# Hybrid SSD, RWKV-7 and mLSTM layer: a later shuffle and more row tiles in the RWKV part, B and C made there, two branch gates between the last mLSTM heads, layer norm copies on two engines

## The chip, the cores and the metric

The kernel runs on 1 core of one Trainium2 chip. The metric is the device time in microseconds (us) of one execution; the time before is the median of three runs. Engine names are those of the profile: PE is TensorE (PEld its weight loads), DVE is VectorE, ACT is ScalarE, POOL is GpSimd, SP is SyncE, which only issues DMAs here.

## The reference: what is computed

One decoder layer over 256 positions of 2048 channels, all float32. `h` is the layer norm of the input. One projection `w_in` feeds three causal mixers and three sigmoid gates; the gated sum of the three branches goes through `w_out`, and a gated MLP with a short causal convolution follows.

```python
def hybrid_mixer(h, w_in, ...):
    proj = h @ w_in
    (ssd_z, ssd_xbc, ssd_dt, rwkv_p, ml_qk, ml_v, ml_o, ml_i, ml_f,
     gate_pre) = jnp.split(proj, IN_SPLITS, axis=-1)
    ...
    g_ssd, g_rwkv, g_mlstm = jnp.split(jax.nn.sigmoid(gate_pre), N_BRANCHES, axis=-1)
    merged = (g_ssd * (y_ssd @ proj_ssd) + g_rwkv * (y_rwkv @ proj_rwkv)
              + g_mlstm * (y_mlstm @ proj_mlstm))
    return merged @ w_out

def reference(x, ...):
    h = layer_norm(x, ln_in_g, ln_in_b)
    h = layer_norm(DEEPNORM_ALPHA * h + hybrid_mixer(h, ...), ln1_g, ln1_b)
    return layer_norm(DEEPNORM_ALPHA * h + conv_ffn(h, ...), ln2_g, ln2_b)
```

In the SSD mixer (Mamba-2), the columns `xbc` go through a convolution of width 4 and a SiLU, and are split into x, B and C; B and C are 512 columns each. The RWKV-7 mixer keeps a 64x64 state in each of 32 heads, with its update `S_t = S_(t-1) diag(w_t) + (S_(t-1) a_t) b_t^T + v_t k_t^T` and `y_t = S_t r_t`. The mLSTM has 8 heads with a running maximum.

## The kernel before, in words

**Weights.** The kernel streams every weight matrix once from HBM. A chunk (`wraw`) holds two row tiles, that is 2 x 128 rows of 512 columns. ACT casts it to the high half `whi` (L163 in the RWKV part, L239 elsewhere), DVE subtracts to get the low half `wlo` (L164, L240), and PE multiplies hi by hi, lo by hi and hi by lo, each in a reduced float32 format. A block of 512 columns has 16 row tiles. In `cm_units` (L256, L258, L260; the result has channels on the partitions) a row tile is 12 matmuls of 128x256; in `tm_units` (L278 to L280; time on the partitions) it is 6 matmuls of 128x512. "Tile" below is such a row tile.

**Layer norm to channels.** `to_cm` transposes the normalised rows on PE (L309), scales into the high half on ACT (L314), scales again into a copy `tocm` on DVE (L315) and subtracts to get the low half `xl` (L317). It runs twice: ahead of `w_in` and ahead of the FFN. `affine_tm` multiplies and adds the norm's vectors to the rows that stay in time order, on POOL (L360), with vectors that SP loads as `gb`.

**The RWKV part** stands in a `manual_schedule`: PE, DVE, ACT and POOL run in the order in which the program issues. Two generators are zipped: `groups()` issues the steps of four groups of heads and yields a number, and for each such number so many elements of `weights()` are issued: one tile of a block, or nothing (`yield False`) while a block waits for a page of SBUF. So each `yield n` puts n tiles of weights between two steps. `weights()` walks through `order`: the k, v and r blocks of groups 1 to 3, then gates, 26 blocks of 16 tiles. A v block's result needs the page that the tail of the group two before has read. `Ahead` loads four chunks ahead and cuts so that two chunks (four tiles) beyond the one in use are cut.

For each group g: `pre(g)` makes decay, a, and the normalised k (LoRA matmuls L628, head sums L670, `nk` L684 and L685); `pairs(g)` makes the pair matrices (L741) and transposes bk (L752); `inverse(g)` inverts a triangular matrix: DVE transposes it (L770), POOL runs a chain of small steps (L783, L785), the shuffle (L808) and two stream transposes (L810, L812) on DVE take its result, and PE goes on with it (L823, L833). Inside that generator stand also the transposes of v (L791), and the norm of k times v (L797 to L806). `tail(g-1)`, woven into it, normalises the group before and transposes it (L925 to L955; PE at L945). `recurrence(g)` is PE's (L856, L867).

**After it.** `ssd_bc` makes B and C: a `cm` block each, the first step of the convolution on ACT (L384), three more for each of four column tiles on DVE (L387), a SiLU on ACT (L969). Then the SSD groups, the projections of RWKV and SSD with their gates (`branch`, merged on POOL at L1146), the mLSTM (`ml_in`, `ml_head`: matmuls L1092, L1093 and L1104; the transposes of its result `mn` at L1158), its projection, `w_out`, and the FFN. In these parts a scheduler orders the instructions by their dependences. A gate's block ends in a sigmoid (L1130) and a store to DRAM on ACT's queue (L1131); `branch` loads it again.

The lines of the changed kernel lie some 10 to 31 further on: L628 is L659 there, L752 is L783, L770 is L801, L808 to L812 are L839 to L843, L823 is L854, L925 to L955 are L956 to L986, L384 is L390, L387 is L396, L1158 is L1180, L1104 is L1126, L360 is L363, and L583 is the new SiLU of B and C.

## Time and profile before

| what | value |
|---|---|
| time, median of 3 runs | 2452.67 us (2452.11 to 2454.07) |
| the profiled execution, its own time | 2451.87 us |
| its span (first to last instruction) | 2450.1 us |
| mean granted clock of PE | 0.984 |
| PE busy | 2369.3 us (97%) |
| DVE, ACT, POOL busy | 1546.7, 1247.3, 509.5 us |
| DMA | 447.66 MB, mean 183 GB/s |

How to read the profile: one execution on the chip was recorded. An engine is busy from the start of an instruction to its end; time between is idle, and the trace names what released the engine (`L164` is line 164 of the kernel, `wlo` the tile). "PE acc L279 <- DVE wlo L164" reads: PE's matmul of line 279 waited for the subtraction of line 164 on DVE. PEclk is the share of full clock that TensorE was granted; 0.5 is half. In a table of stretches each row is from:to in us, then length, PE busy, the number of PE instructions, granted clock, DMA share and GB/s.

### The profile page before, as it was taken

What the parts mean: (1) busy time and instruction counts of PE and PEld (TensorE: products, weight loads), DVE (VectorE), ACT (ScalarE), POOL (GpSimd) and SP (SyncE); (2) the same over time, 40 slices, a digit from 0 to 9 for tenths busy, and PEclk for the clock granted to TensorE, in tenths of its full rate; (3) what the DMA queues carried; (4) which work ended last, traced back from release to release, by engine and by line L of the source; (5) the groups of instructions that cost most, each with busy time, mean ns of one, the idle gap of its engine ahead of it and who ended that gap; (6) DMA issues with size and microseconds to landing.
All of it is one profiled execution on the core that took longest, in us unless ns stands there. A gap on an engine that the chain in (4) does not pass through costs nothing.

```text
span 2450.1 us, 41499 instructions
## 1 busy us (share of the span) xinstructions
PE 2369.3 (97%) x16602; PEld 2131.2 (87%) x16602; DVE 1546.7 (63%) x1856; ACT 1247.3 (51%) x1648; POOL 509.5 (21%) x512
## 2 busy tenths in 40 slices
PE   7999998999999999999999998999999999999997
PEld 7898797798777899998889987787999999998886
DVE  6685575676674566786555666557766666665445
ACT  4554654556464555665434566444555455454333
POOL 0046255264363011423010001301200000000000
PEclk9899999999999999999999999999999999999999
DMA  8445454555565776665766664755655655557664
GB/s 241 144 147 164 140 158 147 154 155 164 148 186 164 213 229 179 183 190 190 263 218 188 174 181 155 238 190 175 189 182 185 185 181 182 186 169 234 194 195 148
DMA packets 283730, 447.66 MB, mean 183 GB/s; under 512 B 25816, under 2 KB 118416, under 8 KB 283152
## 3 DMA queue, kind: packets, MB, share of 16 engines
q1 hardware_dynamic: 280368, 433.99, 58.1%
q10 hardware_dynamic: 2592, 8.91, 0.9%
q8 instruction: 130, 2.13, 0.4%
q0 software_dynamic: 576, 2.10, 0.2%
q14 instruction: 64, 0.52, 0.1%
HBM read 430.19 MB, written 14.72 MB: 182 GB/s over the span
## 4 chain that ended last, share of the span: by engine, by line
PE 83%; POOL 6%; DVE 4%; ACT 3%; DMA 2%; issue 2%; SPq 0%; DVEq 0%; ACTq 0%; POOLq 0%
PE acc L256 13%; PE acc L260 13%; PE acc L258 13%; PE acc L278 13%; PE acc L279 12%; PE acc L280 12%; POOL yi L785 3%; POOL si L783 2%; POOL res L360 1%; DVE wlo L164 1%; PE mix L741 1%; ACT whi L163 1%; DVE wlo L240 1%; PE mix L628 1%; PE mix L1023 1%
## 5 line engine op out<-in xcount | busy, mean ns | idle before, releaser
L240 DVE TENSOR_TENSOR wlo<-wraw,whi 128x1024 fp32r<-128x1024 f32 (+2 forms) x548 | 703.3, 1284 | 519.5 <-ACT whi L239 514.2
L239 ACT CAST whi<-wraw 128x1024 fp32r<-128x1024 f32 (+2 forms) x548 | 569.6, 1041 | 656.5 <-PE acc L280 298.9
L256 PE MATMUL acc<-xh,whi 128*128 128x256 f32 x3104 | 885.1, 286 | 4.9 <-ACT whi L239 2.9
L260 PE MATMUL acc<-xh,wlo 128*128 128x256 f32 x3104 | 881.3, 284 | 5.0 <-DVE wlo L164 4.5
L258 PE MATMUL acc<-xl,whi 128*128 128x256 f32 x3104 | 880.9, 284 | 2.8 <-DVE xl L317 2.8
L256 PEld LDWEIGHTS acc<-xh,whi 128*128 128x128 f32 x3104 | 597.3, 193 | 9.2 <-ACT whi L239 3.5
L260 PEld LDWEIGHTS acc<-xh,wlo 128*128 128x128 f32 x3104 | 596.9, 192 | 7.9 <-DVE wlo L164 5.8
L258 PEld LDWEIGHTS acc<-xl,whi 128*128 128x128 f32 x3104 | 597.7, 193 | 4.8 <-DVE xl L317 3.7
L164 DVE TENSOR_TENSOR wlo<-wraw,whi 128x1024 fp32r<-128x1024 f32 x208 | 278.6, 1351 | 239.1 <-ACT whi L163 238.9
L163 ACT CAST whi<-wraw 128x1024 fp32r<-128x1024 f32 x208 | 216.7, 1049 | 118.3 <-PE acc L280 58.3
L279 PE MATMUL acc<-wlo,xh 128*128 128x512 f32 x640 | 255.5, 399 | 9.9 <-DVE wlo L164 9.8
L278 PE MATMUL acc<-whi,xh 128*128 128x512 f32 x640 | 262.1, 414 | 0.1
L280 PE MATMUL acc<-whi,xl 128*128 128x512 f32 x640 | 253.9, 397 | 0.0
L279 PEld LDWEIGHTS acc<-wlo,xh 128*128 128x128 f32 x640 | 122.9, 192 | 34.5 <-DVE wlo L164 12.0
L278 PEld LDWEIGHTS acc<-whi,xh 128*128 128x128 f32 x640 | 122.4, 191 | 29.5 <-issue 1.2
L280 PEld LDWEIGHTS acc<-whi,xl 128*128 128x128 f32 x640 | 122.9, 192 | 26.3
L279 PE MATMUL acc<-wlo,ah 128*128 128x512 f32 x322 | 125.4, 389 | 0.2 <-DVE wlo L240 0.2
L280 PE MATMUL acc<-whi,al 128*128 128x512 f32 x322 | 125.3, 389 | 0.0
L1236 POOL TENSOR_TENSOR fc<-fc 128x512 f32<-128x512 f32 (+1 forms) x22 | 27.9, 1268 | 453.0 <-DVE fc L387 445.0
L278 PE MATMUL acc<-whi,ah 128*128 128x512 f32 x322 | 111.9, 389 | 0.0
L785 POOL TENSOR_TENSOR yi<-yi,si 128x126 f32<-128x126 f32 (+22 forms) x124 | 84.9, 684 | 9.7
L387 DVE SCALAR_TENSOR_TENSOR fc<-acc,fcols,fc 128x255 f32<-128x255 f32 (+1 forms) x172 | 77.0, 478 | 14.0 <-ACT fc L384 12.5
(357 smaller groups left out, 3025.6 us busy)
## 6 DMA issues: line engine op xcount, KB each, us to landing
wraw<-in_w_in SPq DMA_DIRECT2D x368, 512.0 KB, 3.7
wraw<-in_ffn_w_up SPq DMA_DIRECT2D x336, 256.0 KB, 3.0
wraw<-in_ffn_w_down SPq DMA_DIRECT2D x84, 512.0 KB, 4.4
wraw<-in_proj_rwkv SPq DMA_DIRECT2D x32, 512.0 KB, 4.2
wraw<-in_proj_ssd SPq DMA_DIRECT2D x32, 512.0 KB, 4.5
wraw<-in_proj_mlstm SPq DMA_DIRECT2D x32, 512.0 KB, 4.5
wraw<-in_w_out SPq DMA_DIRECT2D x32, 512.0 KB, 4.2
gdram<-gate ACTq DMA_DIRECT2D x16, 512.0 KB, 3.4
```

The source lines that it names most:

```text
L163: nc.scalar.copy(out=hi, in_=self.raw[i])
L164: nc.vector.tensor_tensor(out=lo, in0=self.raw[i], in1=hi.bitcast(F32), op=ALU.subtract)
L239: nc.scalar.copy(out=hi[:, :n, :width], in_=r)
L240: nc.vector.tensor_tensor(out=lo[:, :n, :width], in0=r, in1=hi[:, :n, :width].bitcast(F32), op=ALU.subtract)
L256: nc.tensor.matmul(a, lhsT=wh[:, o:o + m], rhs=X.h(kt), start=st, stop=False, skip_group_check=True)
L258: nc.tensor.matmul(a, lhsT=wh[:, o:o + m], rhs=X.l(kt), start=False, stop=False, skip_group_check=True)
L260: nc.tensor.matmul(a, lhsT=wl[:, o:o + m], rhs=X.h(kt), start=False, stop=kt == nkt - 1, skip_group_check=True)
L278: nc.tensor.matmul(acc[tt], lhsT=X.h(kt)[:, s], rhs=wh, start=kt == 0, stop=False)
L279: nc.tensor.matmul(acc[tt], lhsT=X.h(kt)[:, s], rhs=wl, start=False, stop=False)
L280: nc.tensor.matmul(acc[tt], lhsT=X.l(kt)[:, s], rhs=wh, start=False, stop=kt == nkt - 1)
L387: nc.vector.scalar_tensor_tensor(out=dst[:, j:], in0=ps[:, :T - j], scalar=v(wname, (width - 1 - j) * nch + ct), in1=dst[:, j:], op0=ALU.m ...
L785: gps.tensor_tensor(out=Yo[:, j + 1:32, :e], in0=Yo[:, j + 1:32, :e], in1=tv, op=ALU.subtract)
```

## The change

- `to_cm`: the copy `tocm` has four buffers, not two; PSUM banks come from two tags in turn; of the two column tiles of a step the first is scaled on ACT, the second on DVE.
- `groups()` starts with `yield 8`: eight tiles come ahead of `pre(0)`.
- In `pre` two tiles become three ahead of `nk`; in `inverse` three become four ahead of the norm's sums, and 24 become 27 ahead of the shuffle; in `tail` four become five ahead of the transposes.
- B and C are two new blocks at the end of `order`; `bc_units` issues their convolutions and SiLU in the hand-written order. `ssd_bc` is gone.
- The gates (2, 2) and (2, 3) leave that order and are issued, as ordinary blocks, after heads 6 and 7 of the mLSTM, with pages of their own.
- `affine_tm(r, "ln1")` is issued after the POOL product of the FFN's step c == 8, no longer ahead of the FFN's first matmul.

```diff
     def to_cm(self, n, gname, bname, X):
-            ps = self.bank().rearrange("p (a t) -> p a t", a=2)
+            ps = self.bank("seq" if kt % 4 else "mix").rearrange("p (a t) -> p a t", a=2)
...
-            tmp = self.pg("s%d" % (kt // 2 % 2), [P, 2, T], "tocm")
+            tmp = self.pg("s%d" % (kt // 2 % 4), [P, 2, T], "tocm")
...
-                nc.vector.tensor_scalar(out=tmp[:, a], in0=ps[:, a], scalar1=g, scalar2=b,
-                                        op0=ALU.mult, op1=ALU.add)
+                if a:
+                    nc.vector.tensor_scalar(out=tmp[:, a], in0=ps[:, a], scalar1=g, scalar2=b,
+                                            op0=ALU.mult, op1=ALU.add)
+                else:
+                    nc.scalar.activation(out=tmp[:, a], in_=ps[:, a], func=AF.Identity, scale=g, bias=b)
...
+    last_gates = [(2, 2), (2, 3)]
+
+    def bc_units(self, nm):
+        cts, _ = yield from self.cm_units(self.a["w_in"], [(0, COL[nm], 512)], [(P * j, P) for j in range(4)],
+                                          self.X)
+        while ("pairs", 3) not in self.done:
+            yield False
+        i = "BC".index(nm)
+        t = self.p4(i, "bc")
+        for j in range(4):
+            self.conv_first(cts[j], t[:, j], "scw", 24, 16 + 4 * i + j, 4, "scb", self.v)
+        for j in range(4):
+            yield False
+            self.conv_rest(cts[j], t[:, j], "scw", 24, 16 + 4 * i + j, 4, self.v)
+        yield False
+        self.nc.scalar.activation(out=t, in_=t, func=AF.Silu)
+        self.BC.append(t)
...
-        later = [(i, j) for i in (0, 2, 3) for j in range(NB)]
+        later = [(i, j) for i in (0, 2, 3) for j in range(NB) if (i, j) not in self.last_gates]
...
-        order += [(1, 3)] + later
+        order += [(1, 3)] + later + [("B", 0), ("C", 0)]
...
         def groups():
+            yield 8
             yield from self.pre(0)
...
         self.split(nrr[:, 0], nrr[:, 1], nr)
-        yield 2
+        yield 3
...
         vec.tensor_tensor(out=sql, in0=sq, in1=sqh.bitcast(F32), op=ALU.subtract)
-        yield 3
+        yield 4
...
-        yield 24
+        yield 27
         vec.stream_shuffle(out=Yc[:, :, :, 1], in_=Yo, mask=[i % 16 + 16 for i in range(32)])
...
         vec.tensor_tensor(out=yv, in0=yv, in1=sv.unsqueeze(2).to_broadcast([P, 16, 64]), op=ALU.mult)
-        yield 4
+        yield 5
...
                 self.ml_head(h, qk[h // 4][:, h % 4], qk[2 + h // 4][:, h % 4], Y)
+                if j == 3:
+                    whole(self.gate_units(*self.last_gates[h % 2], page=10 + h % 2))
...
         self.acb = self.p4(18, "acb")
-        self.ssd_bc()
...
         self.to_cm(lambda tt, j: r[j][:, tt], "ln1_g", "ln1_b", X)
-        self.affine_tm(r, "ln1")
...
-            nc.gpsimd.tensor_tensor(out=u, in0=u, in1=t[1][:, :n], op=ALU.mult)
+            m = nc.gpsimd.tensor_tensor(out=u, in0=u, in1=t[1][:, :n], op=ALU.mult)
+            if c == 8:
+                with self.tc.issue_after(m.ins):
+                    self.affine_tm(r, "ln1")
```

Where the edits move instructions, the engines' order in the compiled program shows it. First DVE at the inverse of group 1, where the tail of group 0 is woven in. Before, subtractions of weights (L164) stand between the steps of the tail (L925 to L933) and the norm (L799):

```order
L164 TENSOR_TENSOR wlo_3710<-wraw_3669,whi_3709 128x1024
L770 STREAM_TRANSPOSE ni_3742<-dg_3737 128x1024
L164 TENSOR_TENSOR wlo_3814<-wraw_3707,whi_3813 128x1024
L925 TENSOR_REDUCE hsm_3829<-yt_2647 128x16
L926 TENSOR_SCALAR hsm_3829<-hsm_3829 128x16
L927 TENSOR_TENSOR yt_2647<-yt_2647,hsm_3829 128x1024
L164 TENSOR_TENSOR wlo_3866<-wraw_3811,whi_3865 128x1024
L799 TENSOR_TENSOR sql_3882<-sq_2968,sqh_3881 128x1024
L164 TENSOR_TENSOR wlo_3902<-wraw_3863,whi_3901 128x1024
L933 TENSOR_REDUCE hsm_3929<-y2_3896 128x16
L164 TENSOR_TENSOR wlo_3934<-wraw_3899,whi_3933 128x1024
```

After, from the same transpose on (L801; the tail is L956 to L986):

```order
L801 STREAM_TRANSPOSE ni_3892<-dg_3887 128x1024
L956 TENSOR_REDUCE hsm_3961<-yt_2743 128x16
L957 TENSOR_SCALAR hsm_3961<-hsm_3961 128x16
L958 TENSOR_TENSOR yt_2743<-yt_2743,hsm_3961 128x1024
L830 TENSOR_TENSOR sql_3984<-sq_3076,sqh_3983 128x1024
L964 TENSOR_REDUCE hsm_3989<-y2_3986 128x16
L837 TENSOR_TENSOR v_2150<-v_2150,mix_3992 128x512
L837 TENSOR_TENSOR v_2150<-v_2150,mix_3998 128x512
L968 RECIPROCAL hsm_3989<-hsm_3989 128x16
L969 TENSOR_TENSOR yt_2743<-yt_2743,hsm_3989 128x1024
L985 TENSOR_TENSOR yo_4006<-yo_4006,v_1406 128x1024
L986 TENSOR_TENSOR yo_4006<-yo_4006,gg_3162 128x1024
```

What moved: the subtractions are gone from among these steps. They stand together, two ahead of the transpose and the next behind L986 and the v block's last steps.

Next ACT at B. Before, in `ssd_bc`, the casts of the chunks of C (L239) stand between the first steps of the convolution (L384) and the SiLU (L969):

```order
L384 ACTIVATE bc_8874<-acc_8632,cst_81 128x256
L239 CAST whi_8956<-wraw_8954 128x1024
L384 ACTIVATE bc_8874<-acc_8633,cst_81 128x256
L239 CAST whi_8986<-wraw_8984 128x1024
L384 ACTIVATE bc_8874<-acc_8632,cst_81 128x256
L239 CAST whi_9016<-wraw_9014 128x1024
L384 ACTIVATE bc_8874<-acc_8633,cst_81 128x256
L239 CAST whi_9046<-wraw_9044 128x1024
L239 CAST whi_9076<-wraw_9074 128x1024
L969 ACT_TABLE_LOAD
L969 ACTIVATE bc_8874<-bc_8874 128x1024
L239 CAST whi_9106<-wraw_9104 128x1024
```

After, in the RWKV part, between B's first steps (L390) and its SiLU (L583), with the tail of group 3 (L961, L966) among them:

```order
L163 CAST whi_8529<-wraw_8493 128x1024
L296 CAST yrh_11266<-yl_11283 128x512
L390 ACTIVATE bc_8557<-acc_8250,cst_81 128x256 x2
L390 ACTIVATE bc_8557<-acc_8251,cst_81 128x256 x2
L961 ACTIVATE y2_8562<-yt_7903 128x1024
L966 ACT_TABLE_LOAD
L966 ACTIVATE hsm_8570<-hsm_8570,cst_81 128x16
L583 ACT_TABLE_LOAD
L583 ACTIVATE bc_8557<-bc_8557 128x1024
L163 CAST whi_8584<-wraw_8527 128x1024
```

What moved: `whi_8529` is C's second chunk and `whi_8584` its third; no cast stands between the two.

Last PE at the mLSTM's last two heads. Before, the transposes of head 6's result (L1158), the next head's scores (L1092, L1093) and products (L1104) stand with few weight matmuls among them:

```order
L280 MATMUL acc_14905<-whi_14981,yml_12818 128x512
L280 MATMUL acc_14906<-whi_14981,yml_12818 128x512
L1158 MATMUL mix_14628<-cst_81,mn_14598 128x128
L1092 MATMUL mix_14798<-mqk_13325,mqk_13845 128x256
L1093 MATMUL mix_14798<-mqk_13325,mqk_13845 128x128
L1158 MATMUL mix_14628<-cst_81,mn_14598 128x128 x3
L1104 MATMUL mix_14806<-mvt_14637,mes_14802 128x258
L1104 MATMUL mix_14806<-mvt_14638,mes_14802 128x258
```

After, around the first transpose of the last head's result (L1180), with the matmuls of the third projection (L278 to L280) ahead of it and behind it:

```order
L279 MATMUL acc_14905<-wlo_14964,ymh_12515 128x512
L280 MATMUL acc_14905<-whi_14963,yml_12517 128x512
L278 MATMUL acc_14906<-whi_14963,ymh_12515 128x512
L279 MATMUL acc_14906<-wlo_14964,ymh_12515 128x512
L280 MATMUL acc_14906<-whi_14963,yml_12517 128x512
L278 MATMUL acc_14905<-whi_14981,ymh_12516 128x512
L279 MATMUL acc_14905<-wlo_14982,ymh_12516 128x512
L280 MATMUL acc_14905<-whi_14981,yml_12518 128x512
L1180 MATMUL mix_14736<-cst_81,mn_14706 128x128
L278 MATMUL acc_14906<-whi_14981,ymh_12516 128x512
```

What moved: the heads' steps stand apart, with the tiles of the two gates and of the projection between them.

More of the change, by code (lines that the diff above doesn't have):

```diff
@@ L46 @@
 C_GATE = C_MI + 16
-COL = {"r": C_R, "k": C_K, "v": C_V}
+COL = {"r": C_R, "k": C_K, "v": C_V, "B": C_B, "C": C_C}
 def gate_column(i, j):
@@ L382, in conv, with conv_first, conv_rest @@
     def conv(self, ps, dst, wname, nch, ct, width, bname, v=None):
-        nc, v = self.nc, v or self.v
-        nc.scalar.activation(out=dst, in_=ps, func=AF.Identity,
-                             scale=v(wname, (width - 1) * nch + ct), bias=v(bname, ct))
+        self.conv_first(ps, dst, wname, nch, ct, width, bname, v or self.v)
+        self.conv_rest(ps, dst, wname, nch, ct, width, v or self.v)
+    def conv_first(self, ps, dst, wname, nch, ct, width, bname, v):
+        self.nc.scalar.activation(out=dst, in_=ps, func=AF.Identity,
+                                  scale=v(wname, (width - 1) * nch + ct), bias=v(bname, ct))
+    def conv_rest(self, ps, dst, wname, nch, ct, width, v):
+        nc = self.nc
         for j in range(1, width):
@@ L556, in rkv_units @@
         self.t[nm, g] = t
+    last_gates = [(2, 2), (2, 3)]
[14 more added lines that the diff above has]
+        self.BC.append(t)
     def rwkv(self):
         nc, tc, W = self.nc, self.tc, self.a["w_in"]
-        self.t, self.g_, self.done = {}, {}, set()
+        self.t, self.g_, self.done, self.BC = {}, {}, set(), []
         self.lw = self.load_lora(0)
@@ L585, in weights @@
                     yield from self.rkv_units(g, "r", 0, ("pairs", g - 1))
+                elif a in ("B", "C"):
+                    yield from self.bc_units(a)
                 else:
@@ L958, in tail @@
         yield 1
-    def ssd_bc(self):
-        nc, W = self.nc, self.a["w_in"]
-        self.BC = []
-        for i, c0 in enumerate((C_B, C_C)):
-            cts, _ = self.block_cm(W, c0, self.X)
-            t = self.p4(i, "bc")
-            for j in range(4):
-                self.conv(cts[j], t[:, j], "scw", 24, 16 + 4 * i + j, 4, "scb")
-            nc.scalar.activation(out=t, in_=t, func=AF.Silu)
-            self.BC.append(t)
     def ssd_group(self, g, Y):
@@ L1122, in ml_head, with gate_units @@
             self.split_scaled(ps[:, i], self.v("ml_nw", ct), Y.h(ct), Y.l(ct))
-    def gate_units(self, i, j):
+    def gate_units(self, i, j, page=18):
         acc = yield from self.tm_units(self.a["w_in"], gate_column(i, j), self.X)
-        g = self.pg("p18", [P, 2, 512], "gate")
+        g = self.pg("p%d" % page, [P, 2, 512], "gate")
         for tt in range(2):
```

## Prediction

> **What bounds the kernel now.** I read the page first, then the waits of TensorE, then a table of stretches around the longest of those waits. The page's rows are the busy time of PE, its granted clock in 40 slices and the chain that ended last:
>
> ```profile
> PE 2369.3 (97%) x16602; PEld 2131.2 (87%) x16602; DVE 1546.7 (63%) x1856; ACT 1247.3 (51%) x1648; POOL 509.5 (21%) x512
> PEclk9899999999999999999999999999999999999999
> PE 83%; POOL 6%; DVE 4%; ACT 3%; DMA 2%; issue 2%; SPq 0%; DVEq 0%; ACTq 0%; POOLq 0%
> ```
>
> PE is busy for 2369.3 of 2450.1 us, so some 81 us are all that better order can win in idle time, and the slower clock after a wait adds to that. The matmuls stay the same in number. The change can only close waits of PE or open new ones. PE's waits (engine, what it waited for, us in total, times, longest):
>
> ```profile
> PE acc L279 <- DVE wlo L164: 9.8, 4, 4.8
> PE seq L823 <- DVE x L810: 5.7, 1, 5.7
> PE mix L1158 <- DVE mn L1116: 5.0, 1, 5.0
> PE mix L1158 <- POOL merged L1146: 3.1, 1, 3.1
> PE acc L258 <- DVE xl L317: 2.8, 3, 1.4
> PE mix L309 <- DVE tocm L315: 2.7, 3, 1.1
> PE mix L528 <- DVE s_gs L514: 1.8, 1, 1.8
> ```
>
> The table of stretches gives start and end, length, PE busy with its count, granted clock, DMA share and GB/s:
>
> ```profile
> 91.60:111.90 20.30, 15.52 (x73) 0.66 0.32 106
> 228.50:241.10 12.60, 9.29 (x82) 0.59 0.39 126
> 349.20:404.70 55.50, 47.12 (x379) 0.97 0.54 162
> 404.70:411.80 7.10, 7.03 (x76) 0.51 0.35 88
> 535.70:541.50 5.80, 4.02 (x21) 0.71 0.59 165
> 617.50:626.80 9.30, 7.71 (x54) 0.82 0.55 170
> 752.90:766.80 13.90, 9.10 (x81) 0.63 0.56 189
> 1500.80:1525.70 24.90, 17.30 (x75) 0.86 0.56 167
> 1554.80:1562.10 7.30, 4.25 (x16) 0.77 0.81 262
> 1691.10:1731.00 39.90, 31.93 (x231) 0.91 0.40 110
> 1800.00:1900.00 100.00, 100.00 (x836) 1.00 0.60 185
> 2300.00:2400.00 100.00, 100.00 (x443) 1.00 0.61 194
> ```
>
> The last two rows give the price of a row tile. A tile of 12 matmuls (channel-major) costs 12 x 100/836 = 1.44 us, one of 6 (token-major) 6 x 100/443 = 1.35 us. Each other row is a wait and its wake: length less busy is idle, and the clock costs between busy x (1 - clock) and length x (1 - clock).
>
> **The change part by part.**
>
> *Later shuffle, groups 0 and 3.* The shuffle needs GpSimd's chain, and two stream transposes follow it. DVE's rows at group 3 (start, us, in brackets the idle time before and who ended it):
>
> ```profile
> 751.60 0.01 DVE L808 LOAD_MASK_SELECT yi<-yi  x1 [4.63 <-POOL yi L785]
> 751.60 1.30 DVE L808 STREAM_SHUFFLE yi<-yi 128x512 f32<-128x512 f32 x1
> 752.94 2.00 DVE L810 STREAM_TRANSPOSE x<-yi 128x1024 f32<-128x1024 f32 x1
> 754.84 1.85 DVE L812 STREAM_TRANSPOSE xt<-yi 128x1024 f32<-128x1024 f32 x1
> ```
>
> DVE stands 4.63 + 5.1 us, and the subtractions that make the low half of the weights are queued behind. Two chunks are cut ahead, four tiles, 5.8 us, and PE runs dry. In program order group 0 now has 32 instead of 28 tiles between the norm and the inverse, group 3 has 43 instead of 39 tiles from the last bk transpose: 5.8 us more for POOL, above the 4.63 waited. What stays is 5.1 us of DVE, under the 5.8 us of lead. Group 0: idle 3.3 and clock 3.8 to 5.2, I take 7.5 (4 to 8). Group 3: idle 4.8 and clock 3.4 to 5.1, I take 9 (4 to 9.5).
>
> *The same in group 1: a loss.* Between the last bk transpose and the inverse 23 tiles stand now, 30 before. The v block has used up its 16 tiles, its page waits for the tail of group 0, and no tile stands until that tail's transposes.
>
> ```profile
> 355.11 2.10 DVE L770 STREAM_TRANSPOSE ni<-dg 128x1024 f32<-128x1024 f32 x1 [1.04 <-ACT dg L768]
> 373.62 1.23 DVE L954 TENSOR_TENSOR yo<-yo,v 128x1024 f32<-128x1024 f32 x1 [2.84 <-POOL si L783]
> 401.23 0.01 DVE L808 LOAD_MASK_SELECT yi<-yi  x1 [8.44 <-POOL yi L785]
> ```
>
> The stretch 349.2 to 404.7 ends by GpSimd (8.44 us of DVE waiting for it), so it keeps its length with less put into it: 7 x 1.44 = 10.1 us of weights move behind it. The tail's chain from 355.11 to 373.62 tells where the hole is. It could be less, if the chain shortens with fewer subtractions on DVE, or more if the clock is low behind the hole: -10 (-6 to -14).
>
> *Small steps (one tile more ahead of the nk matmuls, the norm and the tail).* The rows at 535.7 and 617.5 hold 1.8 + 1.6 us of idle and 2.6 to 3.4 of clock. One tile (1.44 us) covers most: +6 (2 to 7).
>
> *Eight tiles ahead of the first pre().* The row at 91.6 holds 4.8 us idle and 5.3 to 6.9 of clock. The eight tiles (11.5 us) go between and behind the small matmuls, so LoRA matmuls no longer stand with nothing behind them. The 1.8 us wait of L528 and some clock may stay: +7.5 of 10.1 (5 to 10). Why some clock: at 535.7 a single wait of 1.8 us was enough for a mean clock of 0.71. [...]
>
> *B and C in the RWKV stretch.* Their matmuls move, at no price. What they bring is a convolution and a SiLU in the hand-written order. Rows of before, where the scheduler spread the same steps:
>
> ```profile
> 893.32 0.56 ACT L384 ACTIVATE bc<-acc,cst 128x256 f32<-128x256 f32 x1
> 905.00 1.28 ACT L969 ACT_TABLE_LOAD   x1
> 906.29 1.06 ACT L969 ACTIVATE bc<-bc 128x1024 f32<-128x1024 f32 x1
> 907.25 1.03 ACT L239 CAST whi<-wraw 128x1024 fp32r<-128x1024 f32 x1
> 893.45 1.23 DVE L240 TENSOR_TENSOR wlo<-wraw,whi 128x1024 fp32r<-128x1024 f32 x1
> 894.59 1.38 DVE L387 SCALAR_TENSOR_TENSOR bc<-acc,cst,bc 128x253 f32<-128x253 f32 x3
> ```
>
> B's SiLU stands on ACT ahead of the cast of C's third chunk, and waits for 12 convolution steps (4 x 1.38 = 5.5 us) with a reduction among them (about 1.2, an estimate from the subtraction's row). The table loads (1.28 each) are over by then. That is 0.6 for the first step on ACT, 5.5 and 1.2, 7.3 in all; SiLU 1.06, cast 1.03 and subtraction 1.23 make 10.6 us after B's last matmul. PE has C's first four tiles, 5.8 us, so it idles some 4 us and then meets a low clock (4.5, as at 228.5): -8.5 (-3 to -12). With two gates fewer, the SSD's first loads of acb come into the last recurrence, on SP between weight loads; they wait for the last gate's store, and ACT's exponentials for them. Before:
>
> ```profile
> 879.96 0.69 ACT L1015 ACTIVATE es<-acb,atm 128x128 f32<-128x128 f32 x2 [2.71 <-DMA acb<-acd]
> ```
>
> ACT waited 2.71 us there and PE did not. Now a cast for B's last chunks stands behind: 0 to -3, I take 0, as four tiles are cut (5.8 us).
>
> *Two gates between the last mLSTM heads.* At 1500.8 PE stands 7.6 us for the last two heads and loses 2.4 to 3.5 to the clock; 16 token-major tiles after each of them (21.7 us) are free of the heads' chains: +10 (7 to 11). The gates' stores stand on ACT's queue behind their sigmoids, and nothing reads them before the third branch. GpSimd then ends the input norm's multiplies under the last gate and the merge isn't queued among them: the row at 1554.8 goes, 3.05 idle and 1.0 to 1.7 of clock: +4 (2 to 5).
>
> *Layer norm copies on two engines.* To_cm's waits are 2.7 + 2.8 us (L315, L317), and 2.9 of clock in the row at 1691.1 (busy x 0.09). Four buffers and two banks' tags take most, the first wait of the FFN stays: +5 (0 to 9).
>
> *The affine step under the FFN.* GpSimd's eight operations move under convolutions. Rows of before, GpSimd's and DVE's:
>
> ```profile
> 1704.65 6.12 POOL L360 TENSOR_TENSOR res<-res,gb 128x1024 f32<-128x1024 f32 x2 [4.41 <-DMA gb<-in_ln_g]
> 1708.43 3.43 DVE L240 TENSOR_TENSOR wlo<-wraw,whi 128x1024 fp32r<-128x1024 f32 x1
> ```
>
> Beside such an operation a subtraction took 3.43 us (1.23 alone), and a chunk of two tiles lasts 2.88. Eight by 3.06 us are 24.5: with one convolution step (1.38/3 = 0.46) to a chunk DVE falls back by 24.5 x (1 - 2.88/3.89) = 6.4 us, and the lead of 5.8 takes nearly all. On SP the loads of gb stand among the weights' now, and each next pair waits until GpSimd is through with the one before (2 x 3.06); four chunks loaded ahead, 11.5 us, cover that: -0.5 (-6 to 0). [...]
>
> **Sum.** 7.5 + 9 + 6 + 7.5 + 14 + 5 = 49 won; 10 + 8.5 + 0.5 = 19 lost: 30 us. The profiled run took 2451.87 us (span 2450.1), 0.8 below the median of three, 2452.67: 2422.
>
> **Rivals.**
> *The losses hide* (0.14). GpSimd's chain shortens, as DVE has fewer subtractions in it, and C's wait is covered. For it: DVE waits 8.44 us for that chain. Against it: no subtraction can be early where chunks run only two ahead. All 49 are won: 2403.
> *The clock falls again behind each hole left* (0.2). For it: 0.51 to 0.66 in the rows after single waits. Group 1 loses 7 more (as the row at 91.6), the small matmuls keep 5, group 0 wins 4 less: 30 - 16 = 14, so 2438.
> *Slower: the clock stays low while tiles come one by one* (0.05). In group 1's remaining 21 tiles and C's last 8 each chunk could come just in time, at half clock: 29 x 1.44 = 42, less 4.5 counted with C, 37 more: 2459. It decides against the change from 24 tiles at half clock on (30 + 4.9 us). Against it: the longest low stretch in the trace is 20.3 x 0.34/0.5 = 14 us, ten tiles. [...]
> *The order moves and the waits move with it* (0.05). GpSimd's chain gives way by as much as the shuffle is late; then 30 of the 49 stay out: 2452, no change.
>
> **How the numbers follow.** The forecast has 0.56. The range runs from 2404, near the first rival, to 2441, past the second with its error; the last two, 0.1, and a part of the first are left out. Faster by over 0.2% (4.9 us, about what a measurement can tell from no change): 0.56 + 0.14 + 0.2 = 0.9; same 0.05; slower 0.05.
>
> **What would show it.** Right: no waits of L854 or of tiles on the shuffle in groups 0 and 3; PE idle for 12 to 18 us between the bk transposes and the inverse of group 1; 3 to 5 us at C's third chunk; none between the last heads; full clock at the former 91.6. Wrong: a wait of more than 5 us behind FFN's affine, tiles at half clock over 14 us, or waits on loads (wraw) that SP holds behind acb or gb.

## The result, and the profile after

The changed kernel takes 2469.14 us (median of 4 runs, 2462.66 to 2471.31); the kernel before, run beside it, 2452.7. The ratio is 1.0062, with a 95% interval of 1.0042 to 1.0082: slower by 16 us, where 30 us faster was forecast. The profiled execution took 2470.7 us, its span 2468.9, 18.8 more than before. The four runs lie 8.7 us apart, so differences of 2 or 3 us between medians below are not clear of noise.

The page's rows of the changed kernel for the busy time and the granted clock:

```profile
PE 2371.1 (96%) x16602; PEld 2132.7 (86%) x16602; DVE 1532.7 (62%) x1840; ACT 1258.0 (51%) x1670; POOL 507.6 (21%) x512
PEclk9999998999999999999999999999999999999999
```

PE is busy 1.8 us longer than before (2369.3), with as many matmuls, so 17.0 of the 18.8 us are idle time. Its waits in the changed kernel (L1180 was L1158, L898 was L867, L836 was L805, L976 was L945):

```profile
PE acc L279 <- DVE wlo L164: 15.7, 7, 8.4
PE acc L260 <- DVE wlo L164: 8.5, 10, 1.5
PE mix L1180 <- POOL merged L1168: 7.6, 1, 7.6
PE acc L256 <- ACT whi L163: 7.5, 3, 6.3
PE acc L256 <- ACT whi L239: 7.2, 2, 3.6
PE seq L898 <- ACT rsb L890: 5.5, 3, 1.8
PE mix L836 <- ACT sqh L828: 4.4, 1, 4.4
PE seq L976 <- DVE yt L969: 2.4, 1, 2.4
```

Three waits that the change was to remove are gone or short: L823 for the inverse (5.7) and L528 for `s_gs` (1.8) are gone, L1158 for `mn` (5.0) is down to 0.8. In their place PE waits for weights: for the RWKV part's halves (L163, L164) 31.7 us, 16.0 before in the page's waits of L279, L260 and L256. The stretches that answer to those of before (from:to, length, PE busy, clock, DMA share, GB/s):

```profile
110.00:119.00 9.00, 9.00 (x65) 1.00 0.50 152
361.80:419.00 57.20, 40.84 (x278) 0.84 0.39 117
866.00:880.00 14.00, 7.20 (x39) 0.76 0.39 120
1550.00:1566.00 16.00, 8.45 (x34) 0.79 0.65 192
1868.00:1882.00 14.00, 9.89 (x60) 0.76 0.56 166
```

The LoRA matmuls now run at full clock without a wait (first row). Group 1 from the last bk transpose to the inverse has 16.4 us of idle, 8.4 before. The other three rows are new holes: at C's third chunk, at the merge, and in the FFN's seventh step (the expectations call it the third).

To find where time came and went, I took from each trace the start of the same matmuls (landmarks), and subtracted 0.1196 us for each channel-major and 0.2258 for each time-major weight matmul ahead of them (the stretches of before without a wait, 1800 to 1900 and 2300 to 2400 us, hold 836 and 443 matmuls in 100 us). What is left is time lost up to there, whatever blocks stand ahead; the table gives it against the kernel before (us, plus is lost). It is my working from the traces' rows, one trace to a column; the other columns are experiments below. Kernels with the same order up to a landmark differ there by up to 1.6 us (changed and r first), so single entries are good to some 2 us.

| landmark | changed | before + 8 tiles | changed, no 8 | changed, 24 | changed, r first | all repairs |
|---|---|---|---|---|---|---|
| end of group 0's k block | 4.8 | 1.6 | 4.5 | 4.7 | 4.7 | 1.5 |
| first nk matmul, group 0 | -5.5 | -8.4 | 4.0 | -5.6 | -5.6 | -8.5 |
| last bk transpose, group 0 | -0.4 | -4.5 | 4.8 | -2.0 | -2.0 | -4.6 |
| recurrence, group 0 | -6.6 | -5.9 | -2.1 | -4.2 | -8.2 | -10.7 |
| last bk transpose, group 1 | -1.9 | -4.8 | 4.2 | -5.3 | -2.0 | -3.2 |
| recurrence, group 1 | 9.4 | -0.5 | 7.4 | 1.2 | -9.3 | -11.2 |
| recurrence, group 2 | 17.1 | 2.6 | 16.5 | 4.1 | -4.7 | -12.1 |
| recurrence, group 3 | 13.4 | 2.9 | 11.3 | 3.2 | -11.9 | -16.8 |
| first mLSTM head | 22.2 | 4.0 | 21.1 | 12.4 | -8.6 | -12.4 |
| last head's result | 11.6 | 3.7 | 10.4 | 2.0 | -19.2 | -23.2 |
| FFN's first transpose | 16.7 | 3.3 | 13.3 | 5.1 | -13.7 | -27.8 |
| FFN, sixth step | 8.6 | -0.3 | 5.2 | -3.0 | -22.2 | -34.3 |
| FFN, ninth step | 16.2 | -0.3 | 12.0 | 3.8 | -15.9 | -34.3 |
| end | 18.8 | 0.8 | 15.1 | 7.6 | -14.4 | -33.5 |

The first column already shows the shape: gains where they were forecast (10.3 us at the small matmuls, 6.2 at group 0's inverse, 10.6 at the mLSTM heads, 8.1 at the FFN's transposes), and losses between them. The first row is a loss of the new `to_cm` in the prologue: with `to_cm` as before it is some 3 us less (1.5 and 1.6).

Group 1 in the changed kernel, DVE's rows (start, us; in brackets the idle time before and its releaser):

```profile
366.50 1.92 DVE L801 STREAM_TRANSPOSE ni<-dg 128x1024 f32<-128x1024 f32 x1 [1.24 <-ACT dg L799]
...
400.59 1.29 DVE L164 TENSOR_TENSOR wlo<-wraw,whi 128x1024 fp32r<-128x1024 f32 x1 [1.58 <-ACT whi L163]
408.83 0.01 DVE L839 LOAD_MASK_SELECT yi<-yi  x1 [6.95 <-POOL yi L816]
408.83 1.28 DVE L839 STREAM_SHUFFLE yi<-yi 128x512 f32<-128x512 f32 x1
410.14 2.01 DVE L841 STREAM_TRANSPOSE x<-yi 128x1024 f32<-128x1024 f32 x1
412.04 1.87 DVE L843 STREAM_TRANSPOSE xt<-yi 128x1024 f32<-128x1024 f32 x1
413.76 1.58 DVE L562 SCALAR_TENSOR_TENSOR r<-acc,cst,r 128x255 f32<-128x255 f32 x4
415.25 3.50 DVE L164 TENSOR_TENSOR wlo<-wraw,whi 128x1024 fp32r<-128x1024 f32 x3
```

There is no subtraction between 401.9 and 415.25: DVE stands 6.95 us at the shuffle for GpSimd, then does the shuffle, two transposes and the end of the r block. PE's wait of 8.4 us (L279 for `wlo`) is this. Before, PE's wait of 5.7 us for `x` stood here and no tile was left ahead of the inverse.

The experiments' names: "r first" swaps two weight blocks in groups 2 and 3; "queue repairs" are two edits on GpSimd's order; all are shown below.

### The profile page after: what moved, and what is told of

The parts are those of the page before. It is cut to its first block, busy times and chain, and to the rows that moved or that the text cites. A ratio compares the mean times of both kernels' runs of the same rounds, so it can differ in the third digit from the quotient of the medians.

```text
span 2468.9 us, 41471 instructions
## 1 busy us (share of the span) xinstructions
PE 2371.1 (96%) x16602; PEld 2132.7 (86%) x16602; DVE 1532.7 (62%) x1840; ACT 1258.0 (51%) x1670; POOL 507.6 (21%) x512
## 4 chain that ended last, share of the span: by engine, by line
PE 60%; DMA 2%; DVE 1%; POOL 1%; ACT 0%; issue 0%; SPq 0%; DVEq 0%; ACTq 0%; POOLq 0%
PE acc L260 10%; PE acc L256 10%; PE acc L258 10%; PE acc L279 9%; PE acc L280 9%; PE acc L278 9%; DMA wraw<-in_ffn_w_down 1%; PE mix L1043 1%; DMA gb<-in_ln_g 0%; DVE wlo L240 0%; POOL res L363 0%; PE mix L1126 0%; PE mix L1180 0%; DMA wraw<-in_proj_mlstm 0%; DMA gb<-in_ln_in_b 0%
## 5 line engine op out<-in xcount | busy, mean ns | idle before, releaser
L239 ACT CAST whi<-wraw 128x1024 fp32r<-128x1024 f32 (+2 forms) x548 | 569.3, 1041 | 661.5 <-PE acc L280 302.7
L256 PE MATMUL acc<-xh,whi 128*128 128x256 f32 x3104 | 888.8, 287 | 14.6 <-ACT whi L163 7.5
L260 PE MATMUL acc<-xh,wlo 128*128 128x256 f32 x3104 | 881.9, 285 | 10.8 <-DVE wlo L164 8.5
L256 PEld LDWEIGHTS acc<-xh,whi 128*128 128x128 f32 x3104 | 595.6, 192 | 19.7 <-ACT whi L163 8.1
L260 PEld LDWEIGHTS acc<-xh,wlo 128*128 128x128 f32 x3104 | 594.0, 192 | 15.3 <-DVE wlo L164 10.7
L164 DVE TENSOR_TENSOR wlo<-wraw,whi 128x1024 fp32r<-128x1024 f32 x208 | 273.4, 1327 | 259.9 <-ACT whi L163 259.3
L163 ACT CAST whi<-wraw 128x1024 fp32r<-128x1024 f32 x208 | 216.6, 1050 | 126.6 <-PE acc L258 59.7
L279 PE MATMUL acc<-wlo,xh 128*128 128x512 f32 x640 | 255.9, 400 | 15.7 <-DVE wlo L164 15.7
L278 PE MATMUL acc<-whi,xh 128*128 128x512 f32 x640 | 259.4, 412 | 0.0
L280 PE MATMUL acc<-whi,xl 128*128 128x512 f32 x640 | 254.5, 398 | 0.0
L279 PEld LDWEIGHTS acc<-wlo,xh 128*128 128x128 f32 x640 | 122.6, 192 | 41.3 <-DVE wlo L164 19.1
L278 PEld LDWEIGHTS acc<-whi,xh 128*128 128x128 f32 x640 | 122.6, 192 | 29.1 <-issue 1.5
L280 PEld LDWEIGHTS acc<-whi,xl 128*128 128x128 f32 x640 | 122.5, 191 | 26.1
L1256 POOL TENSOR_TENSOR fc<-fc 128x512 f32<-128x512 f32 (+1 forms) x22 | 27.8, 1265 | 536.4 <-DVE fc L396 414.6
L279 PE MATMUL acc<-wlo,ah 128*128 128x512 f32 x322 | 125.5, 390 | 1.1 <-DVE wlo L240 1.1
L280 PE MATMUL acc<-whi,al 128*128 128x512 f32 x322 | 125.3, 389 | 0.0
L278 PE MATMUL acc<-whi,ah 128*128 128x512 f32 x322 | 112.2, 390 | 1.0 <-ACT whi L239 1.0
L814 POOL TENSOR_TENSOR si<-yi,ni 128x126 f32<-128x126 f32 (+22 forms) x124 | 80.5, 649 | 34.3 <-DVE ni L801 18.4
```

The lines of the kernel that those rows point to most:

```text
L163: nc.scalar.copy(out=hi, in_=self.raw[i])
L164: nc.vector.tensor_tensor(out=lo, in0=self.raw[i], in1=hi.bitcast(F32), op=ALU.subtract)
L239: nc.scalar.copy(out=hi[:, :n, :width], in_=r)
L256: nc.tensor.matmul(a, lhsT=wh[:, o:o + m], rhs=X.h(kt), start=st, stop=False, skip_group_check=True)
L260: nc.tensor.matmul(a, lhsT=wl[:, o:o + m], rhs=X.h(kt), start=False, stop=kt == nkt - 1, skip_group_check=True)
L278: nc.tensor.matmul(acc[tt], lhsT=X.h(kt)[:, s], rhs=wh, start=kt == 0, stop=False)
```

## Experiments

**1. Are tiles put in early really won?** The kernel before with one edit, and the changed kernel without it:

```diff
         def groups():
+            yield 8
             yield from self.pre(0)
```

> The kernel before with one line more: eight tiles ahead of the first pre(). Theory (the tiles shift the ends of all later weight blocks against the groups' steps): the small matmuls win about 8 us as in the changed kernel, but the v block of group 2 has 4 tiles left, not 12, behind the last bk transpose of group 1, waits for its page there, and group 1 loses 5 to 12 us; some more waits of 2 to 6 us in the pairs of group 0. Time 2446 to 2458. Rival (tiles cost nothing where they are put, the losses come from the other edits): only the 8 us, 2445, and no new wait in groups 0 and 1.

> The changed kernel without the eight tiles ahead of the first pre(); from the tail of group 0 on its order is the changed kernel's, tile for tile. Theory (the v block of group 2 ends at a fixed tile, so a tile put in ahead of it is taken from the stretch behind the last bk transpose of group 1, where PE waits too): the 8 us at the small matmuls are lost, 6 to 9 us come back in group 1, the rest is the same: 2465 to 2472. Rival (the eight tiles are won for good and something else opens group 1's hole): 2475 to 2479.

Before with eight tiles: 2451.56 us, ratio 1.0 (0.999 to 1.0009): nothing. Its stretches:

```profile
90.00:112.00 22.00, 22.00 (x173) 1.00 0.64 194
351.60:403.90 52.30, 41.60 (x320) 0.91 0.46 143
```

The small matmuls' stretch has no wait left, and the table's column shows 10.0 us won there (from 1.6 to -8.4). Group 1's idle is 10.7 us here (8.4 before); PE's waits say by what:

```profile
PE mix L806 <- DVE sql L800: 4.1, 2, 2.4
PE seq L946 <- DVE yt L939: 3.0, 1, 3.0
```

These are the norm and the tail, which now stand with no tiles between them. 3.9 us go in group 0's pairs, 4.3 in group 1, 2.9 in its recurrence: all is given back. (The 3.6 us that the column wins between the FFN's first transpose and its sixth step come from no edit: this trace has the transposes and matmuls of `to_cm` there in another order than before, and a scheduler makes that order.) The changed kernel without its eight tiles takes 2466.27 us (ratio 1.0058, 1.0043 to 1.0073), no slower than with them. At the inverse of group 1 both stand at 10.2 us lost. The reason is in the order: the v block of group 2 ends at the same weight tile in both, and then waits for the page that the tail of group 0 reads. Whatever is issued ahead of that tile elsewhere is missing behind the last bk transpose: up to that tile 12 are left before, 7 with the edit (I expected 4), 8 in the changed kernel without its eight tiles and 2 with them. Moving eight tiles from one place where PE waits to another is worth nothing. The theory holds, the rivals fall.

**2. The page wait taken away.** In groups 2 and 3 the r block goes ahead of the v block; its page is free by then. The same in the kernel before, as a control:

```diff
-            order += [("k", g), ("v", g), ("r", g), (1, g - 1), later.pop(0), later.pop(0)]
+            rv = [("v", g), ("r", g)] if g < 2 else [("r", g), ("v", g)]
+            order += [("k", g)] + rv + [(1, g - 1), later.pop(0), later.pop(0)]
```

> The changed kernel with the r block ahead of the v block in groups 2 and 3, so that no block waits for the tail's page while the inverse of group 1 runs: 40 tiles stand between the last bk transpose and the inverse there, 23 in the changed kernel. Theory (the page wait eats the tiles): the 11 to 13 us that group 1 loses against before are gone, the later groups are shifted once more by 16 tiles and may win or lose 5; 2452 to 2463. Rival (GpSimd's chain starts late and is what costs): group 1 still loses 8 us or more, 2465 to 2471.

> The kernel before with the r block ahead of the v block in groups 2 and 3, nothing else. Theory (the order of the two blocks is a repair of what the change broke: before, the v block's 12 tiles just last until the tail of group 0): no gain in group 1's inverse beyond 3 us, 2448 to 2455. Rival (r first is better in itself): 2438 or less, and group 1 wins 8 us or more.

The changed kernel with r first takes 2435.97 us, ratio 0.9933 (0.9916 to 0.9949): 33 us less than the changed kernel, 16 less than before, and 16 below the theory's range, which had only group 1 in it. In the control the same edit does nothing: 2452.39, ratio 0.9998 (0.9988 to 1.0008). Group 1 with r first, PE's stretch from the last bk transpose to the inverse, and DVE at the shuffle:

```profile
361.70:425.90 64.20, 61.44 (x379) 0.97 0.61 180
```

```profile
416.50 0.01 DVE L840 LOAD_MASK_SELECT yi<-yi  x1
```

2.8 us of idle where the changed kernel has 16.4, and DVE waits for nothing at the shuffle. It was the larger part of the loss: 18.7 us lie in group 1 (9.4 against -9.3), 12 more in groups 2 and 3 and at B, where the blocks' ends fall elsewhere and B comes before the tail of group 3. Those 12 are seen in the landmarks; which block's end makes each of them was not tried.

**3. The later shuffle.** 24 tiles, not 27, in the changed kernel, and in the kernel with r first and the queue repairs:

```diff
-        yield 27
+        yield 24
         vec.stream_shuffle(out=Yc[:, :, :, 1], in_=Yo, mask=[i % 16 + 16 for i in range(32)])
```

> The changed kernel with 24 tiles ahead of the shuffle. Theory (same fixed end: group 0's three tiles go to group 1's stretch, groups 2 and 3 get back the ends of before in part): group 0 and group 3 lose 4 us each again, groups 1 and 2 win 5 to 8: 2463 to 2473. Rival (27 is what broke groups 1 and 2): 2455 or less.

> As the kernel with r first and both queue repairs, but with 24 tiles ahead of the shuffle as before. Theory (27 is what takes DVE's wait for GpSimd out of the way of the weights in groups 0 and 3): the shuffle of groups 0 and 3 costs 6 to 9 us each again, some of it taken back by other ends; 5 to 15 us slower than that kernel. Rival (with r first GpSimd's chain has cover enough): within 3 us of it.

In the changed kernel 24 is better: 2458.78 us, ratio 1.0026 (1.0015 to 1.0037), 10 us less. This lies below the theory's range and above the rival's: group 0 loses 2.4 us again and group 3 gains 3 us less, as expected, but the stretch up to group 1's last bk transpose wins 1.1 us where the changed kernel loses 4.7, group 1 loses 6.5, not 11.3, and its recurrence with group 2 loses 2.9, not 7.7. With r first it is the other way round: 2444.7 us, 15 us slower than with 27 (2429.85). One edit of three tiles costs 10 or wins 15, by the order of two other blocks. By the same landmarks in this second pair, 27 tiles cost 4.8 us between group 1's last bk transpose and its recurrence with the page wait, and win 4.2 without it; behind that, up to group 2's recurrence, they cost 4.8 and win 6.2. The first of the two has the page wait in it; that the second turns for the same reason is not shown.

**4. B and C.** B's convolution and SiLU issued one by one between C's tiles (changed kernel), and B and C back behind the RWKV part (r first, queue repairs):

```diff
+            if nm == "C" and self.steps:
+                self.steps.pop(0)()
...
+        self.steps = [lambda j=j: self.conv_rest(cts[j], t[:, j], "scw", 24, 16 + 4 * i + j, 4, self.v)
+                      for j in range(4)]
+        self.steps.append(lambda: self.nc.scalar.activation(out=t, in_=t, func=AF.Silu))
```

> The changed kernel with B's three convolution steps per column tile and its SiLU issued one by one between the tiles of C. Theory (the cast of C's third chunk stands behind B's SiLU): the 6.3 us wait at C's third chunk goes, with its slow clock, 9 us in all, of which up to 3 stay: about 2461. Rival (the tail of group 3, not B, holds the casts there): a wait of 4 us or more stays at C's tiles, 2466 to 2470.

> As the kernel with r first and both queue repairs, but with B and C made behind the RWKV part by the scheduler, as before; the two gates stay between the mLSTM heads, so the hand-written order has two blocks of 16 tiles fewer. Theory (the tiles of B and C are what fills the last recurrence and the tail of group 3): PE waits in the last 30 us of the RWKV part for 5 to 20 us more, 2435 to 2450. Rival (the scheduler fills the tail with the next tiles anyway, and B's convolution and SiLU are cheaper there): 2425 to 2432.

What the changed kernel does there, DVE's and ACT's rows:

```profile
866.67 2.93 DVE L396 SCALAR_TENSOR_TENSOR bc<-acc,cst,bc 128x255 f32<-128x255 f32 x6
...
873.00 1.23 DVE L164 TENSOR_TENSOR wlo<-wraw,whi 128x1024 fp32r<-128x1024 f32 x1 [3.39 <-ACT whi L163]
```

```profile
869.68 1.28 ACT L583 ACT_TABLE_LOAD   x1 [2.59 <-DVE bc L396]
870.97 1.06 ACT L583 ACTIVATE bc<-bc 128x1024 f32<-128x1024 f32 x1
871.94 2.92 ACT L163 CAST whi<-wraw 128x1024 fp32r<-128x1024 f32 x3
```

The SiLU waits for the convolution, C's third chunk stands behind it, PE waits 6.3 us. Woven, it takes 2461.17 us (ratio 1.004, 1.0025 to 1.0055), 8 us less, with a wait of 1.8 us left: the theory. The two intervals overlap a little, but the trace has the gain in its place: from group 3's recurrence to the first mLSTM head it loses 2.8 us, not 8.8. In the second pair the rival is right: without the move 2425.0, with it 2429.85, both 0.99 of the kernel before run beside them. Without the page wait the move wins nothing; the traces give it a cost of 3 us in that stretch (4.2 us lost against 1.2), which the times can't tell from none.

**5. GpSimd's queue.** The last part of the input norm's affine step goes behind the third branch's first merge; the FFN's affine step is spread over four steps:

```diff
-        self.affine_tm(r, "ln_in")
+        self.affine_tm(r, "ln_in", range(3))
+        with self.tc.issue_after(self.merge0.ins):
+            self.affine_tm(r, "ln_in", [3])
...
-            if c == 8:
+            if c in (8, 10, 12, 14):
                 with self.tc.issue_after(m.ins):
-                    self.affine_tm(r, "ln1")
+                    self.affine_tm(r, "ln1", [(c - 8) // 2])
```

> The changed kernel with two repairs of GpSimd's queue: the FFN's affine step in four parts behind the products of c = 8, 10, 12 and 14, not all behind 8; and the last part of the input norm's affine step issued behind the third branch's first merge. Theory (in-order queues: the FFN's product and the merge stand behind affine operations, ACT's casts behind the product): the 7 us at the FFN's third step go, and of the 7.6 us wait for the merge 5 to 7 go with some clock: 2455 to 2459. Rival (GpSimd and DVE get in each other's way whatever the order): the FFN loses the 7 us in smaller pieces, 2462 to 2468.

2459.7 us, ratio 1.0028 (1.0019 to 1.0037). GpSimd at the merge in the changed kernel:

```profile
1540.20 6.69 POOL L363 TENSOR_TENSOR res<-res,gb 128x1024 f32<-128x1024 f32 x2 [21.51 <-DMA res<-ntm]
1550.59 2.40 POOL L363 TENSOR_TENSOR res<-res,gb 128x1024 f32<-128x1024 f32 x1 [3.70 <-DMA gb<-in_ln_in_g]
1555.00 3.28 POOL L363 TENSOR_TENSOR res<-res,gb 128x1024 f32<-128x1024 f32 x1 [2.00 <-DMA gb<-in_ln_in_b]
1558.23 3.47 POOL L1168 TENSOR_TENSOR merged<-merged,gate 128x512 f32<-128x512 f32 x2
```

and with the repair:

```profile
1546.03 3.53 POOL L1168 TENSOR_TENSOR merged<-merged,gate 128x512 f32<-128x512 f32 x2 [0.32 <-DVE gate L1167]
```

The merge now runs when its input is there, and between the last head's result and the FFN 4.6 us are won where 5.1 were lost. In the FFN the theory fails: the four parts lose 9.0 us, the one lump 7.6. There the changed kernel's chain is GpSimd, ACT, PE:

```profile
1864.02 5.64 POOL L363 TENSOR_TENSOR res<-res,gb 128x1024 f32<-128x1024 f32 x2 [4.92 <-DMA gb<-in_ln_g]
1869.62 1.26 POOL L1256 TENSOR_TENSOR fc<-fc 128x512 f32<-128x512 f32 x1
```

```profile
1870.91 0.62 ACT L296 CAST ah<-fc 128x512 fp32r<-128x512 f32 x1 [7.50 <-POOL fc L1256]
1871.44 2.94 ACT L239 CAST whi<-wraw 128x1024 fp32r<-128x1024 f32 x3
```

The product stands behind two affine operations, ACT's cast of it behind the product, the casts of the weights behind that. Spread, this wait is gone and another comes, on DVE, with three of the four parts:

```profile
1854.39 2.23 DVE L297 TENSOR_TENSOR al<-fc,ah 128x512 fp32r<-128x512 f32 x1 [1.83 <-ACT ah L296]
1856.54 5.68 DVE L240 TENSOR_TENSOR wlo<-wraw,whi 128x1024 fp32r<-128x1024 f32 x3
```

Beside GpSimd's operations a subtraction takes 1.89 us on average (5.68 / 3) instead of 1.23, right where a step's end already needs DVE. What the move costs net, with the affine step ahead of the FFN again:

```diff
         self.to_cm(lambda tt, j: r[j][:, tt], "ln1_g", "ln1_b", X)
+        self.affine_tm(r, "ln1")
```

> The changed kernel with the affine step ahead of the FFN as before. Theory: the 7 us at the FFN's third step are not lost, 3 of to_cm's 8 us are: 2464 to 2466. Rival (only the place of the 7 us changes): 2468 to 2470.

> As the kernel with r first and both queue repairs, but with the affine step ahead of the FFN as before, the new to_cm kept. Theory (beside the FFN's blocks each pair of affine operations locks DVE out at the block's end, 9 us in all, more than it costs beside to_cm): the FFN's steps lose none of the 9, to_cm's 4 to 6 us of gain go in part: 2422 to 2428. Rival (the affine step costs the same wherever it stands): 2428 to 2433.

2465.96 us in the changed kernel (ratio 1.0054, 1.0037 to 1.0071), 3 less than with it moved; 2422.15 against 2429.85 with r first and the spread: 8 less. Both medians lie where the theory has them, but the intervals of each pair overlap (1.0042 to 1.0082 with it moved; 0.9872 to 0.9901 against 0.9883 to 0.9917). The traces decide: ahead of the FFN the step takes back 3 to 4 us of the gain at `to_cm`, beside the FFN's steps it costs 7 to 9, so by the traces the move loses some 3 and 5 us net. What is then left of the gain at `to_cm`, 3.7 and 3.2 us, is no more than the kernel before with eight tiles won there with the old `to_cm` (3.6): that the copies on two engines win anything ahead of the FFN is not shown, since no run has the old `to_cm` with the affine step moved.

**6. The repairs together, and the other edits on them.** R first with both queue repairs; on that, the three small yields undone (3, 4, 5 back to 2, 3, 4), and the eight tiles taken out:

> The changed kernel with r ahead of v in groups 2 and 3 and with both repairs of GpSimd's queue. The places are apart, so the gains should add: 33 us of the order and 9 of the queue from 2469: 2426 (2422 to 2430). Rival (the time won early is given back later, as the kernel before with eight tiles showed): 2432 to 2437.

> As the kernel with r first and both queue repairs, but without the three added tiles ahead of the nk matmuls, the norm and the tail's transposes (2, 3 and 4 as before). Theory (their worth depends only on where the blocks' ends fall): the waits for the rsb copy and for the weights in the groups go or move, and the time lies within 5 us of that kernel's either way. Rival (they cover the 1.2 to 1.8 us waits as intended): 5 to 9 us slower than it.

> As the kernel with r first and both queue repairs, but without the eight tiles ahead of the first pre(). Theory (with no page wait in the way, what the eight tiles win at the small matmuls is kept): that kernel without them is 5 to 10 us slower, 2435 to 2440. Rival (the eight tiles only move the ends of the blocks): within 3 us of it, 2427 to 2433.

Together: 2429.85 us, ratio 0.99 (0.9883 to 0.9917), at the edge of what was expected, since the FFN's part of the queue repair was none. Without the small yields 2429.32: they are worth nothing. Without the eight tiles 2436.49: now that nothing takes them back, they win 6.6 us. The version from all of this has r first, the merge repair, no small yields, `to_cm` as before in the prologue, and the affine step beside the down projection, where a step has no convolutions (the small addition on GpSimd only marks a place in its queue):

```diff
-            if c in (8, 10, 12, 14):
+            if c == FT - 1:
                 with self.tc.issue_after(m.ins):
-                    self.affine_tm(r, "ln1", [(c - 8) // 2])
+                    self.affine_tm(r, "ln1", [0])
...
+            if name and j + 1 < NB:
+                one = self.cp.tile([P, 2], F32, name="mv", bufs=2)[:, 0:1]
+                s = nc.gpsimd.tensor_tensor(out=one, in0=st[:, 1, j, 0:1], in1=st[:, 1, j, 0:1], op=ALU.add)
+                with self.tc.issue_after(s.ins):
+                    self.affine_tm(r, name, [j + 1])
...
-        self.to_cm(blk, "lin_g", "lin_b", self.X)
+        self.to_cm(blk, "lin_g", "lin_b", self.X, False)
```

> Repairs together: r first, the merge ahead of the last input affine, the three small steps undone, the affine step beside the down projection (the first part behind the last product, one behind each block's residual), and to_cm as before in the prologue (as changed ahead of the FFN). Expected from the regions: 2429.3 less 8 in the FFN and 3 in the prologue, 2418 (2414 to 2423). Rival (the affine parts lock DVE there as well): 2424 to 2428.

2418.89 us, ratio 0.9876 (0.9861 to 0.9891): 50 us less than the changed kernel, 32 less than before. From the FFN's sixth step to the end it loses 0.8 us (the table's right column), the changed kernel 10.2. B and C behind the RWKV part, 3 us by the traces of experiment 4, was not tried with it.

## Why the prediction was wrong

**What was right.** The places of most gains and their sizes: small matmuls +7.5, measured 10.3; group 0's inverse +7.5, 6.2; mLSTM heads +10, 10.6. Two losses too: group 1 -10, measured -11.3, with 16.4 us of idle where 12 to 18 was named; B and C -8.5, measured -8.8, though the wait at C's third chunk is 6.3 us where 3 to 5 was named.

**Small steps, +6, and nothing for the stretches beside the edits: the step that failed first.** "One tile (1.44 us) covers most." I priced each added tile at its own place only. The tiles move the ends of all later blocks, and each end brings DVE and ACT work (a lerp, 1.57 us in the rows below, or two sigmoid steps, 1.09, with a table load of 1.28) that then meets the groups' steps. In the stretches for which I had +6 or nothing the changed kernel loses 5.1 us (pairs of group 0), 4.7 (up to the last bk transpose of group 1), 2.1 (its recurrence), 5.6 (group 2) and 0.9 (pairs of group 3): 18.4 in all, so with the 6 that did not come 24 of the 49 us between forecast and profiled run. Which tiles do it the columns say in part: without the eight tiles the pairs of group 0 lose 0.8 us; with 24 tiles ahead of the shuffle the next stretch wins 1.1, and the recurrence of group 1 with group 2 loses 2.9, not 7.7. So the price left out belongs to the eight tiles and to the later shuffle, which was summed at +6.5 (7.5 + 9 - 10) and costs 10 in the changed kernel (experiment 3). The three small steps were undone only on the repaired kernel; there they are worth nothing (0.5 us).

One meeting is in group 2, DVE's rows behind the shuffle, before and in the changed kernel:

```profile
581.28 2.33 DVE L164 TENSOR_TENSOR wlo<-wraw,whi 128x1024 fp32r<-128x1024 f32 x2
583.62 1.66 DVE L553 SCALAR_TENSOR_TENSOR r<-acc,cst,r 128x255 f32<-128x255 f32 x4
```

```profile
597.96 1.57 DVE L562 SCALAR_TENSOR_TENSOR r<-acc,cst,r 128x255 f32<-128x255 f32 x4
599.45 3.48 DVE L164 TENSOR_TENSOR wlo<-wraw,whi 128x1024 fp32r<-128x1024 f32 x3
```

The lerp of the r block (its mix of neighbouring positions, L562) now stands ahead of the subtractions, and PE waits 2.8 us for `wlo` (L279), where before it waited for none. Another is a gate's sigmoid ahead of the copy that PE waits for, ACT's rows in the changed kernel:

```profile
273.00 1.28 ACT L1152 ACT_TABLE_LOAD   x1
274.29 1.09 ACT L1152 ACTIVATE gate<-acc 128x512 f32<-128x512 f32 x2
275.41 0.33 ACTq L1153 DMA_DIRECT2D gdram<-gate  x1
275.78 1.04 ACT L163 CAST whi<-wraw 128x1024 fp32r<-128x1024 f32 x1 [0.40 <-ACT gate L1152]
276.73 0.38 ACT L890 ACTIVATE rsb<-seq 128x256 f32<-128x256 f32 x1
```

PE waits 1.8 us for `rsb` here, in three groups, and before in none. That shifting alone can do it is shown by the kernel before with eight tiles. That each of these stretches has just this cause was not tried one by one.

**Group 1.** The hole was forecast, but as the price of one edit beside others that win. The eight tiles and the hole are one thing: what the first won is gone at group 1's inverse, as the changed kernel without them shows (10.2 us lost in both). My sum had +7.5 in one line and the loss in another, and both were measured, so the numbers are right here; that one pays for the other, and that a block's page decides it, the sum did not say.

**Group 3, +9:** 4.6; two waits for `wlo` of 1.2 and 1.6 us stay.

**The layer norm copies, +5.** 8.1 are won ahead of the FFN, but by the move of the affine step in part (experiment 5), and some 3 are lost in the prologue, which I had priced at nothing.

**The merge, +4: wrong sign, -5.1.** "GpSimd then ends the input norm's multiplies under the last gate." It could not: two of the four pages that it loads into are held by the last heads' values, GpSimd stands 21.5 us for the load of the third, and the merge stood behind both remaining parts. I took the queue for free without asking when each operation ahead of the merge could start.

**The affine step, -0.5: mis-sized, -7.6.** I priced only DVE's slower subtractions, against the lead. The runs show two things: GpSimd's product queued behind the affine operations with ACT's casts behind it, and, when that is taken away, DVE's slow operations at the end of a step (1.89 us a subtraction on average, not 1.23).

The last 2.6 us of the loss come behind the FFN's ninth step; their cause stays open.

**The rivals.** None was right. GpSimd's chain did shorten, as the first had it (40 us from its first to its last step here, 44 before), but the losses did not hide. "The order moves and the waits move with it" came nearest to the mechanism, and put its chance at 0.05 and its price at zero gain, not at a loss; its own reason, a chain that gives way by as much as the shuffle is late, is not what happened. The rival that had the sign, a clock that stays low while tiles come one by one, was not it: the mean clock is 0.984 in both profiles, and the longest half-clock stretch 13.7 us in both. Nor did the first two signs for "wrong" appear as named: PE's wait behind the FFN's affine step is 3.6 us, and no stretch at half clock is longer than 14. They watched the places of the edits, and half of the error lay beside them.

## What to carry to other kernels

In an order written by hand, filler is a fixed sum: a tile put in front of one wait is taken from in front of another, and a block that waits for a page pins how many there are. Before adding some, count the tiles between each step and the next pinned point, and look where the ends of the blocks come to lie; free the pin first (here the swap of two blocks, worth nothing before the change and 33 us after it). And price an operation on an engine's queue by what stands behind it, from the time at which it can start (here the merge stood behind GpSimd's loads and affine parts, and PE waited 7.6 us for it).

## What the runs showed of the hardware

The record of the granted clock in the changed kernel's trace has, before the last matmul, half-clock stretches of 3.4, 6.8, 10.2 and 13.7 us, one to four times the shortest, and no others. Two of the three waits of 1.8 us at `rsb` were followed within 1.2 us by one of 3.4; the third ended at 638.0, and the next such stretch began at 650.1, behind another wait (1.6 us for `nk`). In the last of the repaired kernels less of the time is at half clock: its mean clock is 0.994, 0.984 before. Closing either of the first two waits would then be worth more than its idle time: by my estimate, half of the 3.4 us, 1.7 us more.
